# Strided attention on one core: storing some head groups alone, and scoring group 0 ahead of the second cast

## The chip, the cores and the metric

One core of one Trainium2 chip. The metric is the device time in microseconds (us) of one execution; medians of several fast runs are quoted. An execution is counted as slow, and left out, when it took over 1.5% longer than the fastest one of the same kernel. "The span" is the profiled part of it, some 2 us shorter than the time. Ratios between kernels are the mean time of one kernel's fast runs over that of the other's fast runs of the same rounds, so they are not quite the ratio of the medians quoted. The calls ran on different chips; times are best compared within one call.

## The reference

Every query attends to 16 fixed keys, those at positions 0, 64, 128 and so on:

```python
batch, heads, seq, dim = (8, 12, 1024, 64)      # float32, stride = 64
for i in range(seq):
    attend_positions = np.arange(0, seq, stride)
    q = Q[:, :, i:i + 1, :]
    k = K[:, :, attend_positions, :]
    v = V[:, :, attend_positions, :]
    scores = np.einsum('bhqd,bhkd->bhqk', q, k) * scale
    weights = ...softmax of scores...
    result[:, :, i, :] = np.einsum('bhqk,bhkd->bhqd', weights, v)[:, :, 0, :]
```

Q is 25.2 MB and is read once; the result is 25.2 MB and is written once. The kernel moves some 51 MB and computes little.

## The kernel before

The 96 heads are handled in 24 groups of four, 1 MB of Q and 1 MB of result each. All transfers are issued from one queue (SP), in program order. Ten input buffers let loads 0 to 9 go ahead; load g+10 needs the buffer of group g. A group is cast to bf16 (half on GpSimd, half on ScalarE), transposed on VectorE, scored on TensorE, exponentiated on ScalarE, multiplied with V on TensorE, and scaled by the reciprocal sums on VectorE (five eighths of it) and on ScalarE and GpSimd (the last three eighths).

```python
def cast(g):
    ...
    nc.gpsimd.tensor_copy(out=qb[g][:, 0:half], in_=qn[g][:, 0:half])
    nc.scalar.copy(qb[g][:, half:], qn[g][:, half:])

def store(g, groups, a):                 # a: parity of the head
    o = out_sb[g][a : P : 2]             # every second partition: 64 rows
    _copy(nc,
          _ap_with(out, [[16 * D, 64], [2 * SD, 2 * groups], [1, 16 * D]],
                   g * HG * SD + a * SD),
          _ap_with(o, [o.ap[0], [1, 1], [1, 32 * groups * D]]))

key_rows(0)
cast(0)
cast(1)
keys(0, 0)
transpose(0)
scores(0)
keys(0, 1)
... # V, transpose(1), cast(2)
for g in range(NG):
    ... # outputs(g), and the steps ahead of the next groups
    if g >= NG - 2:
        for a in range(2):
            store(g, 1, a)
    elif g % 2 == 1:
        for a in range(2):
            store(g - 1, 2, a)           # two groups at once, one parity: 16 KiB reads
            if g - 1 + a + QBUFS < NG:
                load(g - 1 + a + QBUFS)
```

Two groups lie side by side in one output buffer, so a store of one parity of both reads 16 KiB from each of 64 partitions. A store of one group reads 8 KiB pieces.

The softmax here doesn't subtract the row's maximum and nothing guards it: scores larger than these inputs give would overflow.

Of the kernel before, what the change touches and what calls it, by code (L numbers as in the profile page):

```python
# [12 lines left out]
BF16 = mybir.dt.bfloat16  # L13
# [6 lines left out]
def _ap_with(ap: bass.AP, new_ap, extra_offset: int = 0) -> bass.AP:  # L20
    return dataclasses.replace(
        ap, ap=[list(p) for p in new_ap], offset=ap.offset + extra_offset
    )


def _copy(nc, out: bass.AP, in_: bass.AP):

    sides = [
        mybir.BassSymbolicTensorAccessPattern(
            ap=side.ap, dtype=side.dtype, bass_ap=side,  # L30
            is_dma=True, for_custom_bir_dma=True,
        )
        for side in (in_, out)
    ]
    return nc.sync.add_instruction(  # L35
        mybir.InstDMACopy(
            name=nc.get_next_instruction_name(), engine=mybir.EngineType.SP,
            ins=sides[:1], outs=sides[1:], queue="qSPDynamicHW",
            mode="Copy",
        )  # L40
    )
# [9 lines left out]
def kernel(  # L51
# [8 lines left out]
    nc = tc.nc  # L60

    B, H, S, D = Q.shape
# [3 lines left out]
    P = 128  # L66
    HG = 4
    NG = B * H // HG
    NC = NG // 2
    SD = S * D  # L70
    KW = P + NK
    assert B * H == NG * HG and S == 1024 and D == 64 and NK == 16
    QBUFS = 10
    OBUFS = 4

    const = ctx.enter_context(tc.tile_pool(name="const", bufs=1))
# [16 lines left out]
    def load(g):  # L93
        qn[g] = qn_pool.tile([P, 32 * D], FP32, name="qn", tag="qn")
        n = P if g < 2 else 32
        _copy(nc, qn[g], _ap_with(Q, [[HG * SD // n, n], [1, HG * SD // n]], g * HG * SD))
# [18 lines left out]
    for c in range(2):  # L115
        for a in range(2):
            for e in range(2):
                nc.gpsimd.tensor_copy(
                    out=perm_v[:, c, a, :, e], in_=id_v[:, c, :, a]
# [4 lines left out]
    w_bufs = []  # L124
    for i in range(3):
        w = const.tile([P, 8, P], BF16, name=f"w{i}")
# [6 lines left out]
        out=slot_i, in0=iota_p, scalar1=4, scalar2=3,  # L133
# [6 lines left out]
        out=s_sel, in0=col4, scalar1=slot_f, scalar2=None, op0=ALU.is_equal  # L140
# [15 lines left out]
    def key_rows(m):  # L156
        part = slice(4 * m, 4 * m + 4)
        nc.scalar.copy(k_bf[:, part], k_raw[:, part])  # L158
        nc.vector.transpose(  # L159
            k_r[:, part].rearrange("p n d -> p (n d)").bitcast(I32),  # L160
            k_bf[:, part].rearrange("p n d -> p (n d)").bitcast(I32),
        )


    def keys(m, c):
        for s in range(4):
            src, dst, col = 32 * (2 * c + s % 2), 32 * (2 * (s % 2) + s // 2), NK + 32 * s
            op = nc.vector.tensor_copy if m == 0 and s >= 2 else nc.scalar.copy
            op(  # L169
                k_t[dst : dst + 32, 8 * m + c : 8 * m + 8 : 2, :, col : col + NK],  # L170
                k_r[src : src + 32, 4 * m : 4 * m + 4].rearrange(
                    "p n (a k f) -> p a n f k", a=2, f=2
                )[:, s // 2],
            )


    def value_rows(n):
        for c in range(2):
            vp = psum_sc.tile([P, NC // 2, D], FP32, name="vp", tag="sc")
            nc.tensor.matmul(  # L180
                vp, lhsT=perm_v[:, c].rearrange("p a b e k -> p (a b e k)"),
                rhs=v_bf[:, 6 * n : 6 * n + 6], start=True, stop=True,
            )
            nc.vector.tensor_copy(out=v_rep[:, 6 * n : 6 * n + 6, c], in_=vp)  # L184

    qb, qt, wt, vb, rec, out_sb, out_2 = {}, {}, {}, {}, {}, {}, {}


    def values(g):
        vb[g] = v_bufs[g % 3]  # L190
        nc.gpsimd.tensor_tensor(  # L191
            out=vb[g][:, 0 : 4 * D].rearrange("p (s d) -> p s d", s=4), in0=mask,
            in1=v_rep[:, g // 2, g % 2].unsqueeze(1).to_broadcast([P, 4, D]),
            op=ALU.mult,
        )

    def cast(g):
        qb[g] = qb_pool.tile([P, 32 * D], BF16, name="qb", tag="qb")
        half = 16 * D
        nc.gpsimd.tensor_copy(out=qb[g][:, 0:half], in_=qn[g][:, 0:half])  # L200
        nc.scalar.copy(qb[g][:, half:], qn[g][:, half:])  # L201

    def transpose(g):
        qt[g] = qt_pool.tile([P, 32 * D], BF16, name="qt", tag="qt")
        nc.vector.transpose(qt[g].bitcast(I32), qb[g].bitcast(I32))  # L205

    def scores(g):
        sc = psum_sc.tile([P, 512], FP32, name="sc", tag="sc")
        q = qt[g]
        for e in range(2):  # L210
            for f in range(2):
                nc.tensor.matmul(  # L212
                    sc, lhsT=k_t[:, g, f, NK * (1 - e) : NK * (1 - e) + P],
                    rhs=_ap_with(
                        q, [q.ap[0], [D, 8], [16 * D, 2], [2, 32]],
                        extra_offset=8 * D * e + f,
                    ),
                    start=e + f == 0, stop=e + f == 2,
                )
        w = wt[g] = w_bufs[g % 3]  # L220
        for a in range(2):
            wa = w[64 * a : 64 * a + 64]
            nc.scalar.activation(  # L223
                out=_ap_with(wa, [wa.ap[0], [P, 8], [4, 32], [2, 2]], extra_offset=a),
                in_=sc[64 * a : 64 * a + 64].rearrange("p (t x q) -> p t q x", t=8, x=2),
                func=AF.Exp, bias=0.0, scale=scale,
            )


    def outputs(g, c):  # L230
        if c == 0:
            if g % 2 == 0:
                out_2[g // 2] = out_pool.tile(
                    [P, 2, 4, 8, D], FP32, name="out_sb", tag="out_sb"
                )
            out_sb[g] = out_2[g // 2][:, g % 2]
            rec[g] = rec_pool.tile([P, 8, 4], FP32, name="rec", tag="rec")
        i0, n = ((0, 3), (3, 2), (5, 3))[c]
        ps = psum_o.tile([P, 3, 512], FP32, name="o_ps", tag="o")
        for i in range(n):  # L240
            nc.tensor.matmul(  # L241
                ps[:, i, 0 : 4 * D + 4], lhsT=wt[g][:, i0 + i], rhs=vb[g],
                start=True, stop=True,
            )
        r = rec[g][:, i0 : i0 + n]
        o = ps[:, 0:n, 0 : 4 * D].rearrange("p i (s d) -> p i s d", s=4)
        to = out_sb[g][:, :, i0 : i0 + n].rearrange("p s i d -> p i s d")
        by = r.unsqueeze(3).to_broadcast([P, n, 4, D])
        nc.vector.reciprocal(r, ps[:, 0:n, 4 * D : 4 * D + 4])  # L249
        if c < 2:  # L250
            nc.vector.tensor_tensor(out=to, in0=o, in1=by, op=ALU.mult)  # L251
        else:
            nc.scalar.copy(to, o)  # L253
            nc.gpsimd.tensor_tensor(out=to, in0=to, in1=by, op=ALU.mult)  # L254


    def store(g, groups, a):
        o = out_sb[g][a : P : 2]
        _copy(
            nc,  # L260
            _ap_with(
                out, [[16 * D, 64], [2 * SD, 2 * groups], [1, 16 * D]],
                g * HG * SD + a * SD,
            ),
            _ap_with(o, [o.ap[0], [1, 1], [1, 32 * groups * D]]),
        )

    key_rows(0)
    cast(0)
    cast(1)  # L270
    keys(0, 0)
    transpose(0)
    scores(0)
    keys(0, 1)
    nc.vector.tensor_copy(out=v_bf, in_=v_raw)
    transpose(1)
    value_rows(0)
    values(0)
    values(1)
    cast(2)  # L280
    def ahead(g):
        if g + 2 < NG:
            transpose(g + 2)
        if g + 1 < NG:
            scores(g + 1)
        if g + 2 < NG:
            values(g + 2)
        if g + 3 < NG:
            cast(g + 3)

    for g in range(NG):
        if g > 0:
            ahead(g)
        for c in range(3):
            outputs(g, c)
        if g == 0:
            ahead(g)
        if g in (1, 5):
            key_rows(g // 4 + 1)
        if g in (2, 3, 6, 7):  # L300
            keys(g // 4 + 1, g % 4 - 2)
        if g == 4:
            value_rows(1)
        if g >= NG - 2:
            for a in range(2):
                store(g, 1, a)
        elif g % 2 == 1:
            for a in range(2):
                store(g - 1, 2, a)
                if g - 1 + a + QBUFS < NG:  # L310
                    load(g - 1 + a + QBUFS)
# [33 lines left out]
```

## Time and profile before

| | before |
|---|---|
| time, median (range) | 132.21 us (132.01 to 132.62), 3 runs |
| span | 130.1 us |
| DMA engines busy, mean of 16 | 96% |
| busiest compute engine | VectorE, 68% |

How to read the profile lines: in the rows of stretches by time, the columns are start and end of the stretch, its length, then busy time and instructions of PE, weight loads, DVE, ACT and POOL, then the granted TensorE clock, the DMA share and GB/s. This view books the bytes of a packet where the packet starts, so a share slightly above 1 means busy throughout. In timeline lines: start, duration, engine, source line, operation, output<-input. For a DMA line, the duration is that of the issue, not that of the transfer. The lines of the kernel before stand in the prediction below.

Beside the views I use the trace's records of single DMA packets, which have a start, a duration and a size, but no number of their engine. Loads from load 2 on consist of 32 KiB packets (median 1219 ns), pair stores of 16 KiB packets (616 ns), and lone stores of 8 KiB packets (311 ns). From them I work out two figures for each run, over the packets that start between 29 and 66 us:

- **idle**: the time in which fewer than 16 packets are in flight, the missing ones summed and divided by 16;
- **excess**: each packet's duration less the median of its size as given here, summed and divided by 16. It is what slow packets cost.

### The profile page before, as it was taken

How to read it: one execution, taken by the hardware profiler on the slowest of the kernel's cores; microseconds unless marked ns; L12 is line 12 of the kernel's file. 1: busy time of each engine (PE TensorE's matmuls, PEld its weight loads, DVE VectorE, ACT ScalarE, POOL GpSimd, SP SyncE). 2: the span in 40 equal slices, each digit the busy share in tenths (PEclk: the TensorE clock that was granted, in tenths of full speed). 3: DMA queues.
4: the chain of work that ended last, by engine and by line, in shares of the span. 5: the costliest groups of instructions: out<-in, count | busy, mean ns of one | idle time of the engine just before them, and what ended most of it. 6: DMA issues, size and time to landing. Idle time of an engine off the chain costs nothing.

```text
span 130.1 us, 1201 instructions
## 1 busy us (share of the span) xinstructions
PE 65.9 (51%) x292; PEld 30.6 (24%) x292; DVE 88.8 (68%) x167; ACT 86.3 (66%) x120; POOL 80.1 (62%) x89
## 2 busy tenths in 40 slices
PE   0000669376885647743667764666646377450000
PEld 0000223133342313321332331333323223210000
DVE  6964565469688968796898797979798865660000
ACT  3133365967899896999978789797979683431000
POOL 8933074918657875785878969696988755244000
PEclk9999999955558996799975699999999955865555
DMA  3999989997979999999999999999999999999991
GB/s 70 353 322 463 474 343 473 423 383 322 322 267 451 388 443 436 393 438 446 408 428 453 398 438 453 388 438 453 393 433 458 388 438 428 423 421 428 403 406 50
DMA packets 6535, 51.20 MB, mean 393 GB/s; under 512 B 3904, under 2 KB 3904, under 8 KB 3904
## 3 DMA queue, kind: packets, MB, share of 16 engines
q1 hardware_dynamic: 6528, 51.12, 96.0%
q8 instruction: 2, 0.03, 0.1%
q14 instruction: 5, 0.04, 0.1%
HBM read 25.95 MB, written 25.17 MB: 393 GB/s over the span
## 4 chain that ended last, share of the span: by engine, by line
DMA 35%; POOL 23%; issue 17%; DVE 5%; ACT 4%; PE 4%; SPq 1%; POOLq 1%; DVEq 0%; ACTq 0%
DMA qn<-in_Q_dram 35%; POOL out_sb L254 9%; POOL qb L200 8%; POOL v L191 5%; DVE out_sb L251 3%; PE sc L212 3%; ACT qb L201 2%; DVE qt L205 1%; POOLq L340 1%; ACT out_sb L253 1%; PE o_ps L241 1%; DVE rec L249 1%; ACT k_t L169 1%; ACT w L223 1%; SPq L35 1%
## 5 line engine op out<-in xcount | busy, mean ns | idle before, releaser
L241 PE MATMUL o_ps<-v,w 128*128 128x260 bf16 x192 | 39.0, 325 | 36.0 <-DVE out_sb L251 31.8
L254 POOL TENSOR_TENSOR out_sb<-out_sb,rec 128x768 f32<-128x768 f32 x24 | 35.3, 1471 | 29.4 <-ACT out_sb L253 29.4
L251 DVE TENSOR_TENSOR out_sb<-o_ps,rec 128x768 f32<-128x768 f32 (+1 forms) x48 | 39.6, 824 | 1.9 <-DVE rec L249 0.3
L212 PE MATMUL sc<-qt,k_t 128*128 128x512 bf16 x96 | 33.2, 481 | 14.0 <-ACT k_t L169 13.5
L223 ACT ACTIVATE w<-sc 64x512 bf16<-64x512 f32 x48 | 35.4, 737 | 5.1 <-PE sc L212 4.7
L205 DVE STREAM_TRANSPOSE qt<-qb 128x1024 int32<-128x1024 int32 x24 | 29.6, 1232 | 12.8 <-POOL qb L200 7.8
L241 PEld LDWEIGHTS <-w 128*128 128x128 bf16 x192 | 19.2, 111 | 59.9 <-DVE out_sb L251 40.4
L201 ACT CAST qb<-qn 128x1024 bf16<-128x1024 f32 x24 | 25.1, 1045 | 7.6 <-DMA qn<-in_Q_dram 7.0
L253 ACT COPY out_sb<-o_ps 128x768 f32<-128x768 f32 x24 | 19.2, 798 | 14.6 <-DVE rec L249 14.3
L200 POOL CAST qb<-qn 128x1024 bf16<-128x1024 f32 x24 | 24.9, 1037 | 5.2 <-DMA qn<-in_Q_dram 5.2
L249 DVE RECIPROCAL rec<-o_ps 128x12 f32<-128x12 f32 (+1 forms) x72 | 15.1, 210 | 7.4 <-PE o_ps L241 6.7
L191 POOL TENSOR_TENSOR v<-mask,v_rep 128x256 bf16<-128x256 bf16 x24 | 16.1, 669 | 3.9 <-DVE v_rep L184 3.9
L212 PEld LDWEIGHTS <-k_t 128*128 128x128 bf16 x96 | 10.9, 114 | 24.9 <-ACT k_t L169 13.5
L169 ACT COPY k_t<-k_r 32x128 bf16<-32x128 bf16 x20 | 5.9, 294 | 0.2
L129 POOL MEMSET k_t<- 128x4608 bf16 x1 | 3.9, 3936 | 0.0
L184 DVE CAST v_rep<-vp 128x384 bf16<-128x384 f32 x4 | 2.1, 538 | 2.0 <-PE vp L180 2.0
L158 ACT CAST k_bf<-k_raw 128x256 bf16<-128x256 f32 x3 | 1.2, 407 | 3.1 <-DMA k_raw<-in_K_dram 3.1
L139 DVE TENSOR_SCALAR s_sel<-col,slot_f 128x4 bf16<-128x4 int16 x1 | 2.5, 2545 | 0.1
L159 DVE STREAM_TRANSPOSE k_r<-k_bf 128x128 int32<-128x128 int32 x3 | 0.9, 308 | 2.3 <-ACT k_bf L158 2.3
L180 PE MATMUL vp<-v_bf,perm_v 128*128 128x384 bf16 x4 | 1.5, 413 | 0.6 <-DVE v_rep L184 0.6
L158 ACT ACT_TABLE_LOAD x1 | 1.3, 1283 | 0.7 <-PEq L326 0.7
L123 DVE MEMSET k_t<- 128x1152 uint32 x1 | 1.0, 1018 | 1.0 <-PEq L326 1.0
(17 smaller groups left out, 6.6 us busy)
## 6 DMA issues: line engine op xcount, KB each, us to landing
qn<-in_Q_dram SPq DMA_DIRECT2D x24, 1024.0 KB, 14.1
out_dram<-out_sb SPq DMA_DIRECT2D x22, 1024.0 KB, 13.6
out_dram<-out_sb SPq DMA_DIRECT2D x4, 512.0 KB, 9.2
k_raw<-in_K_dram SPq DMA_DIRECT2D x1, 384.0 KB, 4.3
v_raw<-in_V_dram SPq DMA_DIRECT2D x1, 384.0 KB, 7.4
```

The source lines that it names most:

```text
L169: op(k_t[dst : dst + 32, 8 * m + c : 8 * m + 8 : 2, :, col : col + NK], k_r[src : src + 32, 4 * m : 4 * m + 4].rearrange("p n (a k f) -> p ...
L191: nc.gpsimd.tensor_tensor(out=vb[g][:, 0 : 4 * D].rearrange("p (s d) -> p s d", s=4), in0=mask, in1=v_rep[:, g // 2, g % 2].unsqueeze(1).t ...
L200: nc.gpsimd.tensor_copy(out=qb[g][:, 0:half], in_=qn[g][:, 0:half])
L201: nc.scalar.copy(qb[g][:, half:], qn[g][:, half:])
L205: nc.vector.transpose(qt[g].bitcast(I32), qb[g].bitcast(I32))
L212: nc.tensor.matmul(sc, lhsT=k_t[:, g, f, NK * (1 - e) : NK * (1 - e) + P], rhs=_ap_with(q, [q.ap[0], [D, 8], [16 * D, 2], [2, 32]], extra_ ...
L223: nc.scalar.activation(out=_ap_with(wa, [wa.ap[0], [P, 8], [4, 32], [2, 2]], extra_offset=a), in_=sc[64 * a : 64 * a + 64].rearrange("p (t ...
L241: nc.tensor.matmul(ps[:, i, 0 : 4 * D + 4], lhsT=wt[g][:, i0 + i], rhs=vb[g], start=True, stop=True,)
L249: nc.vector.reciprocal(r, ps[:, 0:n, 4 * D : 4 * D + 4])
L251: nc.vector.tensor_tensor(out=to, in0=o, in1=by, op=ALU.mult)
L253: nc.scalar.copy(to, o)
L254: nc.gpsimd.tensor_tensor(out=to, in0=to, in1=by, op=ALU.mult)
```

## The change

The intent is to give the DMA queue its first stores earlier. The first four groups, and the last two, are stored alone; and the keys and scores of group 0 are recorded ahead of cast 1, which has to wait for load 1. Nearly every store is one DMA of 1 MB before and after (only the last four were halves), so no DMA is split; what changes is when its data are ready. Lone groups lay the attention weights out differently, so the pairs need three zeroed weight buffers of their own.

```diff
+    def alone(g):
+        return g < 4 or g >= NG - 2
...
-        w = wt[g] = w_bufs[g % 3]
+        w = wt[g] = (w_bufs if alone(g) else w_pair)[g % 3]
+        wa_pos, wa_step = ([[2, 32], [1, 2]], 64) if alone(g) else ([[4, 32], [2, 2]], 1)
...
+    def store(g):                       # 128 rows, 8 KiB reads
+        o = out_sb[g]
+        _copy(nc,
+            _ap_with(out, [[16 * D, P], [2 * SD, 2], [1, 16 * D]], g * HG * SD),
+            _ap_with(o, [o.ap[0], [1, 1], [1, 32 * D]]))
...
     key_rows(0)
+    keys(0, 0)
     cast(0)
+    ...three w_pair tiles, memset on GpSimd...
+    transpose(0)
+    keys(0, 1)
+    scores(0)
     cast(1)
-    keys(0, 0)
-    transpose(0)
-    scores(0)
-    keys(0, 1)
... (transpose(1) moves behind values(1))
-        if g >= NG - 2:
-            for a in range(2):
-                store(g, 1, a)
+        if alone(g):
+            store(g)
+            if g + QBUFS < NG:
+                load(g + QBUFS)
         elif g % 2 == 1:
             for a in range(2):
-                store(g - 1, 2, a)
+                store_two(g - 1, a)     # as before
```

More of the change, by code (lines that the diff above doesn't have):

```diff
@@ L223, in scores @@
             nc.scalar.activation(
-                out=_ap_with(wa, [wa.ap[0], [P, 8], [4, 32], [2, 2]], extra_offset=a),
+                out=_ap_with(wa, [wa.ap[0], [P, 8], *wa_pos], extra_offset=a * wa_step),
                 in_=sc[64 * a : 64 * a + 64].rearrange("p (t x q) -> p t q x", t=8, x=2),
@@ L254, in outputs, with store_two @@
             nc.gpsimd.tensor_tensor(out=to, in0=to, in1=by, op=ALU.mult)
-    def store(g, groups, a):
+    def store(g):
+        o = out_sb[g]
+        _copy(
+            nc,
+            _ap_with(out, [[16 * D, P], [2 * SD, 2], [1, 16 * D]], g * HG * SD),
+            _ap_with(o, [o.ap[0], [1, 1], [1, 32 * D]]),
+        )
+    def store_two(g, a):
         o = out_sb[g][a : P : 2]
@@ L261, in store @@
             _ap_with(
-                out, [[16 * D, 64], [2 * SD, 2 * groups], [1, 16 * D]],
+                out, [[16 * D, 64], [2 * SD, 4], [1, 16 * D]],
                 g * HG * SD + a * SD,
             ),
-            _ap_with(o, [o.ap[0], [1, 1], [1, 32 * groups * D]]),
+            _ap_with(o, [o.ap[0], [1, 1], [1, 64 * D]]),
         )
     key_rows(0)
+    keys(0, 0)
     cast(0)
+    w_pair = []
+    for i in range(3):
+        w = const.tile([P, 8, P], BF16, name=f"w_pair{i}")
+        nc.gpsimd.memset(w, 0.0)
+        w_pair.append(w)
+    transpose(0)
+    keys(0, 1)
+    scores(0)
     cast(1)
-    keys(0, 0)
-    transpose(0)
-    scores(0)
-    keys(0, 1)
     nc.vector.tensor_copy(out=v_bf, in_=v_raw)
-    transpose(1)
     value_rows(0)
@@ L279 @@
     values(1)
+    transpose(1)
     cast(2)
```

## The prediction

> **What bounds the kernel now.** I began with the page: busy shares, the 40 slices, the chain that ended last; then asked for the stretches by time, the timeline, and the DMA queue's own waits. No compute engine is above 68% of the span, but the 16 DMA engines are at 96%:
>
> ```profile
> PE 65.9 (51%) x292; PEld 30.6 (24%) x292; DVE 88.8 (68%) x167; ACT 86.3 (66%) x120; POOL 80.1 (62%) x89
> ...
> GB/s 70 353 322 463 474 343 473 423 383 322 322 267 451 388 443 436 393 438 446 408 428 453 398 438 453 388 438 453 393 433 458 388 438 428 423 421 428 403 406 50
> ...
> q1 hardware_dynamic: 6528, 51.12, 96.0%
> ```
>
> So it is bound by moving 51.12 MB: at the 426 GB/s of the long steady stretch (below) that alone is 120.0 us of the 130.1 us span. The interest is in the other 10. The GB/s row has one hole in the middle: slices 10 to 12 (each 3.25 us) at 322, 322 and 267. The stretches by time, with the last two columns DMA share and GB/s, place it:
>
> ```profile
> 9.00:30.00 21.00, 11.72 (x38) 4.87 (x39) 12.04 (x21) 12.16 (x18) 9.19 (x10) 0.91 1.04 437
> 30.00:32.00 2.00, 0.74 (x5) 0.22 (x3) 1.93 (x5) 1.94 (x3) 1.94 (x3) 0.50 0.31 131
> 32.00:39.00 7.00, 6.11 (x22) 2.73 (x21) 5.32 (x9) 5.98 (x12) 3.83 (x4) 0.50 1.01 311
> 39.00:126.00 87.00, 47.33 (x233) 22.80 (x231) 63.06 (x120) 63.46 (x86) 58.14 (x56) 0.83 1.00 426
> ```
>
> Two different faults lie there. From 30 to 32 us the DMA share is 0.31: the engines are idle. From 32 to 39 us the share is 1.01, but only 311 GB/s move: the engines are busy and slow. The timeline of the DMA queue says why the first one exists:
>
> ```profile
> 2.63 9.71 SPq L35 DMA_DIRECT2D qn<-in_Q_dram  x9
> 30.36 0.63 SPq L35 DMA_DIRECT2D out_dram<-out_sb  x1
> 31.09 0.54 SPq L35 DMA_DIRECT2D qn<-in_Q_dram  x1
> ...
> 39.74 0.59 SPq L35 DMA_DIRECT2D out_dram<-out_sb  x1
> ```
>
> All ten loads that the input buffers allow are issued by 12.34 us. Nothing follows until 30.36 us, because the first store waits for both groups of pair 0, and load 10 stands behind that store in the same queue. In the trace's packet records the last packets of load 9 end between 30.68 and 31.21 us, and the first store packet starts at 31.65. What held the store is the last multiply of group 1 on GpSimd, 28.86 to 30.33 us:
>
> ```profile
> 28.86 1.47 POOL L254 TENSOR_TENSOR out_sb<-out_sb,rec 128x768 f32<-128x768 f32 x1 [2.94 <-ACT out_sb L253]
> ```
>
> From 39 us to the end nothing starves. The chain that ended last runs over GpSimd early, and over loads (35% of the span) later; the waits of the DMA queue for GpSimd after 39 us cost nothing, as the queue has work in hand.
>
> **What the Trainium skill says.** "DMA: Bandwidth & Descriptors", section "Queues, rings and completion order": on each DMA engine descriptors are consumed in ring order. The trace agrees: the loads of the first stage finish one after another, about 2.49 us apart, so a store issued at 20 us is not carried out at 20 us but is ready when load 9 ends. "HBM Reference", section "Specifications (TRN2)": a core streaming alone measures about 425 GB/s, bounded by its 16 DMA engines; the trace has 426. So there is no faster steady rate to win, only holes to close. "Perfetto Trace Analysis", section "DMA Optimizations": splitting DMAs may let some start sooner. That is what storing groups alone does. I found no page that explains a stretch of busy but slow packets.
>
> **The change, part by part.**
>
> *Reads of 8 KiB.* Stores of groups 0 to 3 read 128 rows of 8 KiB where pairs read 64 rows of 16 KiB. In the packet records the median 8 KiB packet takes 311 ns (they are what the last four stores use) and the median 16 KiB packet 616 ns. A group has 64 x 16 KiB, 4 for each engine: 4 x (2 x 311 - 616) = 24 ns. Four groups: +0.1 us. Groups 22 and 23 keep 8 KiB reads, in two issues instead of four: 0.
>
> *Three more zeroed buffers.* Pairs and lone groups lay their weights out differently, so there are three new w buffers, zeroed on GpSimd. The memset of k_t there takes 3.94 us for 4608 columns, 0.855 ns each; 3 x 1024 columns make 2.6 us. They stand between cast 0 (ends 8.78 us) and cast 1, which waits for load 1 until 11.89 us. 8.8 + 2.6 = 11.4: hidden.
>
> *Keys and scores of group 0 ahead of cast 1.* Before, the first score matmul starts at 13.47 us because ACT does cast 1 (11.87 to 12.91, on load 1) ahead of the keys. After, ACT does the keys at about 7.4, cast 0 to about 9.0; the transpose (1.25) ends at about 10.3, and the remaining keys at about 10.7. Scores start near 10.5, 3 us earlier. Values of group 0 on GpSimd still come after cast 1 (12.9) and v_rep (about 13.8), so output matmuls of group 0 start near 14.5, not 17.08: 2.6 us earlier. Before, its last multiply ended at 21.23 + 1.47 = 22.7, so it ends near 20.
>
> *Store 0 and load 10 alone.* The store can go at about 20 us instead of 30.36, ten before the loads run out. Load 10 follows at once. Store 0 and load 10 are 2.1 MB, 4.9 us at 426 GB/s: work until about 30.9 + 4.9 = 35.8. Store 1 is needed by then; it was ready at 30.3 in the kernel before and should be at about 28. Each further group adds 4.9 us of DMA work against 4.5 to 4.9 us between the last multiplies (28.86, 33.73, 38.24, 42.87). Pair 4/5 was ready at 48.15 and is needed at 30.9 + 4 x 4.9 = 50.5, so the return to pairs does not starve either. Idle DMA goes.
>
> *The sum.* Against 426 GB/s the kernel before loses 2 x (1 - 131/426) = 1.4 us in the idle stretch, and 7 x (1 - 311/426) = 1.9 us in the slow one; together 3.3. Nothing else that bounds changes. If both vanish: 132.2 - 3.3 + 0.1 = 129.0. If only the idle one does: 132.2 - 1.4 + 0.1 = 130.9.
>
> **The rivals.** (A) *The slow packets come from restarting dry engines.* For: 16 KiB packets take up to 1306 ns there, about twice the median, and it starts 1.2 us after the restart; packets also run slow (8 KiB in 700 to 800 ns) at 3.8 us, just after the DMA first starts. Against: the first two packets of every engine after the restart run at full speed. Then both parts go, near 129.0.
> (B) *They come from the first writes to the output, whenever those start.* For: the dip follows the first stores, and it hits loads behind them as well; no reads alone show it. Against: later stores go to equally fresh addresses at full speed. Then the slow stretch only moves: near 130.9, or 131.3 if the window boundaries of mine gave the idle part too much.
> (C) *The granted clock or the engines' load slow the DMA.* The clock is 0.50 in that stretch; but it is also 0.50 at 69 to 72 us with 448 GB/s, so I dismiss it.
> (D) *Compute becomes the bound between groups 1 and 5.* Margins of 2 to 8 us as above speak against it; a miss would give back a microsecond.
> (E) *The end is ragged.* The last stores end between 126.5 and 128.6 us, one engine trailing others by up to 2 us. The change does not touch its cause, and it can move the time by 0.5 us either way.
>
> **Range and chances.** I give A and B about equal weight: (129.0 + 130.9) / 2 is 129.95, and I lean a little to the faster side because a partial remedy of the slow stretch is possible even under B, as loads are then mixed in sooner: 129.8. Half a microsecond either side of the two cases makes 128.4 to 131.6. The 2% border is at 129.57: under A about two in three fall below, under B one in ten, so faster 0.39, same 0.59, slower 0.02. Being slower by 2.6 us would need a new hole as large as the present one, and I see none.
>
> **What would show it.** Right: the first store issued near 20 us with load 10 just behind; no stretch between 3 and 125 us with a DMA share under 0.9; first scores near 10.5 us; the span's end earlier by what the hole loses. A stretch around 31 to 37 us at the full rate decides for A; one of busy share near 1 at about 300 GB/s decides for B. Wrong: store 0 issued after 25 us, a second hole near 36 or 50 us because outputs come late, or 8 KiB packets well above 311 ns when mixed with loads.

## The result

| | before | after |
|---|---|---|
| time, median (range) | 132.22 us (132.01 to 132.62), 4 runs | 129.05 us (128.95 to 129.44), 4 runs |
| ratio, 95% interval | | 0.9762 (0.9732 to 0.9793) |
| span | 130.1 us | 127.3 us |
| end of the last DMA packet | 128.63 us | 126.02 us |
| idle, excess (29 to 66 us) | 0.93, 2.13 us | 0.11, 0.20 us |

The changed kernel is 2.4% faster. A second and a third set of runs of it, below, gave 0.9795 (0.9777 to 0.9813) and 0.9770 (0.9740 to 0.9800), so that a gain of 2% is not clear of the noise in these two. The profiled execution of the kernel before took 131.88 us, that of the changed one 129.10: the profiles account for 2.8 us, not for the whole difference of the medians. The stretches by time of the kernel after, over the hole and past it:

```profile
9.00:30.00 21.00, 13.07 (x44) 5.40 (x44) 15.12 (x25) 12.36 (x19) 13.80 (x15) 0.92 1.03 433
30.00:32.00 2.00, 1.45 (x9) 0.57 (x6) 1.97 (x5) 1.69 (x5) 0.84 (x1) 1.00 0.74 307
32.00:39.00 7.00, 3.42 (x18) 1.61 (x19) 5.31 (x12) 6.82 (x12) 5.31 (x6) 0.97 1.03 437
39.00:123.00 84.00, 46.87 (x224) 22.26 (x222) 60.60 (x114) 60.28 (x82) 55.77 (x53) 0.80 1.01 426
```

The stretch from 32 to 39 us went from 311 to 437 GB/s, and the steady rate stayed at 426. The 0.74 from 30 to 32 us is not a hole: by the packet records at least 16 packets are in flight from 29 to 32 us, but few start there. The queue's timeline, and group 0 on its way to the first store:

```profile
2.63 9.61 SPq L35 DMA_DIRECT2D qn<-in_Q_dram  x9
20.61 0.63 SPq L35 DMA_DIRECT2D out_dram<-out_sb  x1
21.34 0.55 SPq L35 DMA_DIRECT2D qn<-in_Q_dram  x1
27.96 0.59 SPq L35 DMA_DIRECT2D out_dram<-out_sb  x1
...
45.84 0.59 SPq L35 DMA_DIRECT2D out_dram<-out_sb  x1
```

```profile
8.63 2.73 POOL L287 MEMSET w_pair<- 128x1024 bf16 x3
10.42 1.87 PE L215 MATMUL sc<-qt,k_t 128*128 128x512 bf16 x4 [10.42 <-DVE qt L208]
11.80 1.36 POOL L203 CAST qb<-qn 128x1024 bf16<-128x1024 f32 x1 [0.44 <-DMA qn<-in_Q_dram]
...
19.11 1.47 POOL L259 TENSOR_TENSOR out_sb<-out_sb,rec 128x768 f32<-128x768 f32 x1 [2.86 <-ACT out_sb L258]
```

Store 0 is issued at 20.61 us instead of 30.36, ten ahead of the end of load 9 (30.41 to 31.08 us over the engines), and load 10 stands right behind it. The memsets are over before cast 1's data are in. They were not quite free: a copy of keys on VectorE, started at 10.40 us, took 1.04 us instead of 0.22 and ended 0.08 us after the last memset. This cost the DMA queue nothing here; the dry spell in the middle, below, shows a profile in which it did.

One line of the table of groups was not in my working, the exponentials, by layout:

```profile
L228 ACT ACTIVATE w_pair<-sc 64x512 bf16<-64x512 f32 x36 | 26.6, 738 | 1.9 <-PE sc L215 1.6
...
L228 ACT ACTIVATE w<-sc 64x512 bf16<-64x512 f32 x12 | 7.1, 591 | 3.7 <-PE sc L215 3.6
```

The lone layout writes neighbouring columns and takes 591 ns, not 738, for the same number of elements. It takes 1.8 us off ScalarE in all, which bounds nothing here.

### The profile page after: what moved, and what is told of

Read it like the earlier page. It is cut to its first block, busy times and chain, and to the rows that moved or that the text cites. A ratio compares the mean times of both kernels' runs of the same rounds, so it can differ in the third digit from the quotient of the medians.

```text
span 127.3 us, 1203 instructions
## 1 busy us (share of the span) xinstructions
PE 64.8 (51%) x292; PEld 29.9 (24%) x292; DVE 89.3 (70%) x167; ACT 84.5 (66%) x120; POOL 83.0 (65%) x92
## 4 chain that ended last, share of the span: by engine, by line
POOL 39%; issue 25%; DVE 11%; DMA 6%; ACT 4%; PE 4%; POOLq 1%; DVEq 0%
POOL qb L203 15%; POOL out_sb L259 14%; POOL v L194 10%; DMA out_dram<-out_sb 6%; DVE qt L208 3%; DVE out_sb L256 3%; PE sc L215 2%; DVE s_sel L139 2%; ACT qb L204 2%; PE o_ps L246 2%; ACT out_sb L258 1%; POOLq L360 1%; DVE w L127 1%; ACT w L228 1%; DVE rec L254 1%
## 5 line engine op out<-in xcount | busy, mean ns | idle before, releaser
L259 POOL TENSOR_TENSOR out_sb<-out_sb,rec 128x768 f32<-128x768 f32 x24 | 35.3, 1471 | 30.1 <-ACT out_sb L258 30.1
L246 PE MATMUL o_ps<-v,w_pair 128*128 128x260 bf16 x144 | 27.7, 305 | 28.1 <-DVE out_sb L256 24.3
L215 PE MATMUL sc<-qt,k_t 128*128 128x512 bf16 x96 | 32.1, 468 | 10.4 <-DVE qt L208 10.4
L228 ACT ACTIVATE w_pair<-sc 64x512 bf16<-64x512 f32 x36 | 26.6, 738 | 1.9 <-PE sc L215 1.6
L246 PEld LDWEIGHTS <-w_pair 128*128 128x128 bf16 x144 | 13.7, 106 | 44.4 <-DVE out_sb L256 30.3
L246 PE MATMUL o_ps<-v,w 128*128 128x260 bf16 x48 | 11.1, 367 | 9.0 <-DVE out_sb L256 8.3
L228 ACT ACTIVATE w<-sc 64x512 bf16<-64x512 f32 x12 | 7.1, 591 | 3.7 <-PE sc L215 3.6
L246 PEld LDWEIGHTS <-w 128*128 128x128 bf16 x48 | 5.2, 120 | 16.6 <-DVE out_sb L256 10.8
L287 POOL MEMSET w_pair<- 128x1024 bf16 x3 | 2.7, 947 | 0.0
```

The lines of the kernel that those rows point to most:

```text
L215: nc.tensor.matmul(sc, lhsT=k_t[:, g, f, NK * (1 - e) : NK * (1 - e) + P], rhs=_ap_with(q, [q.ap[0], [D, 8], [16 * D, 2], [2, 32]], extra_ ...
L228: nc.scalar.activation(out=_ap_with(wa, [wa.ap[0], [P, 8], *wa_pos], extra_offset=a * wa_step), in_=sc[64 * a : 64 * a + 64].rearrange("p ...
L246: nc.tensor.matmul(ps[:, i, 0 : 4 * D + 4], lhsT=wt[g][:, i0 + i], rhs=vb[g], start=True, stop=True,)
L259: nc.gpsimd.tensor_tensor(out=to, in0=to, in1=by, op=ALU.mult)
```

## The experiments

The theory after the result: the whole gain is that the DMA engines no longer run dry. Running dry costs twice, once as idle time and once as a stretch of slow packets after the restart. Rivals: the slow stretch belonged to the first writes to the output; or to the parity pairs; or the earlier scores are worth something of their own.

### Each part alone

The first run takes the order alone, in the kernel before (transpose(1) moves here too):

```diff
     key_rows(0)
+    keys(0, 0)
     cast(0)
+    transpose(0)
+    keys(0, 1)
+    scores(0)
     cast(1)
-    keys(0, 0)
-    transpose(0)
-    scores(0)
-    keys(0, 1)
...
```

> The kernel before with the new order of keys and scores alone; every store stays a parity pair. Main theory (the loss was only that the first store came after the loads had run out, and dry engines restart slowly): group 1 ends at about 27.9 us as in the changed kernel, pair 0 is issued at about 28.0, ahead of the loads' end at 30.4 to 31.1; no stretch from 30 to 39 us under 400 GB/s; 129.1 us. Rival (the first stores must be lone, because 16 KiB pair reads or two parity stores as the first writes are what ran slowly): idle stretch gone, slow stretch of 5 to 6 us stays, about 131.0 us.

The second takes the lone stores alone: the changed kernel with the order of before.

> The changed kernel with the old order of casts, keys and scores; the lone stores stay. Main theory: group 0 ends at about 22.7 us, store 0 is issued then, 8 us ahead of the loads' end; 129.1 us, the same as the changed kernel, so each of the two parts would have been enough alone. Rival (the earlier start of scores is worth something of its own): between 129.6 and 131 us.

| | time | ratio to before (95%) | idle, excess |
|---|---|---|---|
| order alone | 130.03 us | 0.9836 (0.9821 to 0.9850) | 0.12, 1.13 us |
| lone stores alone | 129.94 us | 0.9837 (0.9804 to 0.9870) | 0.12, 0.66 us |
| changed kernel | 129.51 us | 0.9795 (0.9777 to 0.9813) | 0.10, 0.18 us |

Each part alone takes the idle time away and gives about four fifths of the gain of that call. The parts are two remedies for one fault, not two gains. But neither reached the 129.1 us that the main theory expected, and the lone stores came out inside the range of the rival that gave the earlier scores a worth of their own (129.6 to 131). The packet records speak for slow packets instead: some remain, from 32 to 36 us with the order alone and from 52 to 56 us with the lone stores alone. With the order alone:

```profile
32.00:39.00 7.00, 2.92 (x18) 1.45 (x18) 5.43 (x12) 6.80 (x14) 5.57 (x6) 0.96 1.04 396
```

In these two, the store concerned was issued some 2 us ahead of its turn. In the changed kernel it is 4 us or more. The times differ as the excess does (0.48 us of excess and 0.43 us of time between the lone stores and the changed kernel), but the intervals of these two overlap, so this rival is made unlikely and not excluded.

### Loads ahead of the first stores

Loads 10 and 11 need only casts 0 and 1, so they need not stand behind a store:

```diff
+    load(QBUFS)
+    load(QBUFS + 1)
     for g in range(NG):
...
-                if g - 1 + a + QBUFS < NG:
+                if g > 1 and g - 1 + a + QBUFS < NG:
                     load(g - 1 + a + QBUFS)
```

> The kernel before with nothing changed but that loads 10 and 11 are issued ahead of the first stores (they wait for casts 0 and 1 alone, so they can go at about 13 us). The loads then run to about 36 us and the first store, still issued near 30.4 us as a pair, is carried out behind them. Main theory: no dry stretch, no slow one, 129.2 us, perhaps 0.3 more since pair 1 at 39.7 us comes just as pair 0's stores end at 41. Rival (first writes are slow whenever they come as pairs): slow stretch at 36 to 42 us, 130.9 us.

130.89 us, ratio 0.9903 (0.9886 to 0.9920): a miss in the time. The packet records say where it went. The first stores, pair 0 of both parities from 35.3 to 41 us, ran at full speed: their 16 KiB packets took 616 ns, although they were the first writes and pairs. This refutes the rival of the first writes. But pair 1 then came just in time: its first store was issued at 39.24 us, with only the second store of pair 0 still under way, and started at about 40.5 us. Idle was only 0.19 us, yet the excess was 1.87 us, with 16 KiB packets at up to 1245 ns from 41.7 to 43 us and slow 32 KiB packets behind them. The stretches by time of this kernel:

```profile
32.00:39.00 7.00, 4.83 (x22) 2.12 (x20) 5.51 (x11) 6.46 (x14) 4.34 (x4) 0.83 0.97 410
39.00:46.00 7.00, 5.33 (x20) 2.42 (x21) 5.68 (x12) 6.39 (x9) 4.90 (x6) 0.66 1.06 350
```

The slow stretch moved to where the queue was nearly empty; the lower rate stands in the row of 39 to 46 us.

### A hold that held nothing

> The changed kernel with the stores of groups 4 and 5 and the loads 14 and 15 held back until after group 6 (issue near 51 us, not 45.8), so that the DMA engines run dry in the middle, at 50 to 51.6 us, for 1 to 2 us, long after the first writes. If any restart of dry engines brings a slow stretch: idle about 1.4 us plus about 1.9 us of slow packets (16 KiB packets near 1250 ns) from 53 to 59 us, about 132.3 us. If the slow stretch of the kernel before belonged to the first writes or the first phase only: the idle time alone, about 130.5 us, packets at 611 to 616 ns right after the restart.

The edit put the stores of pair 4/5 behind group 6 in the program. On SP a store waits only for the data that it reads, and no other transfer stood ahead of it, so it went out at 45.75 us as ever: 129.51 us and no dry spell. The run tested neither theory. It serves as a second run of the changed kernel, used in the table above.

### Loads further ahead

```diff
+    for g in range(QBUFS, QBUFS + 3):
+        load(g)
...
         if g == 0:
             ahead(g)
+            load(QBUFS + 3)
...
-                if g - 1 + a + QBUFS < NG:
-                    load(g - 1 + a + QBUFS)
+                if g > 1 and g + 1 + a + QBUFS < NG:
+                    load(g + 1 + a + QBUFS)
```

> The kernel before with loads 10 to 13 issued ahead of the first stores and every later load two groups earlier; all stores stay parity pairs. So far the slow packets came in this order: 2.0 us of excess packet time where the store came after the engines were dry (before), 1.7 where it came about 1.5 us ahead of its turn (loads 10 and 11 ahead), 0.7 and 0.4 where it came 2 to 2.5 us ahead (order alone, lone stores alone), none where it came 4 us ahead (changed kernel). If the short lead is what counts: here every pair is issued 6 us or more ahead of its turn, no slow stretch, about 129.6 us. If engines in step (ends of one transfer within 0.6 us over the 16 engines) followed by a pair store and a load are what counts: slow stretch of 1 to 2 us of excess at pair 1, near 46 to 52 us, about 131 us.

130.00 us, ratio 0.9849 (0.9801 to 0.9897), idle 0.11 and excess 0.92 us. The large slow stretch is gone, as the lead theory said, but a mild one is left, from 45.7 to 48.4 us, in the third store in a row (packets of 700 to 970 ns), and that store had been issued six microseconds ahead. So a short lead is not the only condition for slow packets. The rival of this run, engines in step, had expected 1 to 2 us of excess and about 131 us; the result lies between the two and settles neither. What else counts stays open.

### Dry on purpose, with lone stores, and in the middle

To hold a store back in fact, it must stand in the queue behind another that has to wait. First with lone stores:

```diff
         if alone(g):
-            store(g)
-            ...
+            for h in {0: (), 1: (), 2: (2, 0, 1)}.get(g, (g,)):
+                store(h)
+                if h + QBUFS < NG:
+                    load(h + QBUFS)
```

> The changed kernel, but the stores of groups 0 and 1 stand behind the store of group 2 (issue near 32.7 us), so the engines run dry at 30.4 to 31.1 us for about 2.8 us and restart with lone stores of 8 KiB reads. If any restart of dry engines brings a slow stretch: 2.8 us idle plus about 2 us of excess packet time in the 6 us after the restart, near 134.0 us. If slow packets need the parity pairs: idle time alone, packets at 311 ns, near 131.9 us.

134.54 us over the three fast runs (a fourth, 136.65 us, was counted as slow), ratio 1.0179 (1.0126 to 1.0232). Idle 3.52 us, excess 1.61 us: 8 KiB packets took 540 to 669 ns from 36.0 to 37 us, and half of the 32 KiB packets of the load behind them 1581 to 2051. So the slow stretch does not need parity pairs. The same with pair 4/5 behind pair 6/7, in the middle of the run:

```diff
+            for h in {5: (), 7: (7, 5)}.get(g, (g,)):
                 for a in range(2):
-                    store_two(g - 1, a)
+                    store_two(h - 1, a)
...
```

> The changed kernel, but the stores of pair 4/5 stand behind those of pair 6/7, which need group 7 (issue near 55 us): the engines run dry at 50 to 51.6 us for 4 to 5.5 us, in the middle, and restart with a parity pair long after the first writes. If a restart with a parity pair brings the slow stretch: about 5 us idle and 2 us of excess, near 136 us. If the slow stretch belonged to the first phase of the run: 5 us idle alone, near 134 us. (The run e4 was meant to do this, but its stores wait only for their own groups and went out unmoved; it counts as a second run of the changed kernel.)

The profiled run was counted as slow (138.46 us); the three fast ones took 136.30, 136.51 and 136.97 us, and the ratio is 1.0344 (1.0290 to 1.0397). The profile is used for what happens around the dry spell only. Its stretches by time:

```profile
39.00:46.00 7.00, 5.12 (x21) 2.33 (x22) 5.80 (x12) 6.22 (x9) 5.11 (x6) 0.76 0.99 418
46.00:53.00 7.00, 3.35 (x21) 1.77 (x20) 5.99 (x12) 5.78 (x11) 4.76 (x5) 1.00 0.63 261
53.00:59.00 6.00, 3.36 (x18) 1.51 (x17) 3.86 (x8) 5.83 (x11) 4.47 (x5) 0.92 0.11 45
59.00:66.00 7.00, 4.97 (x19) 2.11 (x16) 5.40 (x9) 5.91 (x8) 5.00 (x5) 0.58 1.01 318
```

The engines fell idle between 50 and 52.2 us and stayed so until 58.6 us, and from 59 to 66 us they were busy at 318 GB/s: the picture of the kernel before at 30 to 39 us, 27 us later and long after the first writes. Idle was 8.28 us and excess 2.02 us; the fourth 16 KiB packet of each engine took 1240 to 1295 ns.

The trace shows what set this execution apart from its early stage on. Two lines of GpSimd's timeline, then one of VectorE's:

```profile
7.57 1.04 POOL L203 CAST qb<-qn 128x1024 bf16<-128x1024 f32 x1 [1.03 <-DMA qn<-in_Q_dram]
8.55 2.73 POOL L287 MEMSET w_pair<- 128x1024 bf16 x3
...
7.35 4.00 DVE L169 COPY k_t<-k_r 32x128 bf16<-32x128 bf16 x2
```

The second of these two copies of keys on VectorE started at 7.58 us, 13 ns after cast 0 on GpSimd, and took 3.77 us instead of 0.22: it ended at 11.36 us, 0.08 us after the memsets that follow the cast. In the ten profiles in which the copy started before the cast, it took 0.22 us; in the other two in which it started after, 1.07 us (loads ahead, without memsets) and 3.64 us (lone stores alone). Here the first scores came at 12.69 us, not 10.42, store 0 at 22.88, not 20.61, and the held pair's stores as much later. In the fast runs, which were not profiled, the dry spell was therefore probably about 2.3 us shorter. An estimate from these figures: 129.05 us, 5.9 us more idle and 1.8 us more excess make 136.7 us; without the slow stretch 134.9. The fast runs took 136.3 to 137.0, so they too speak for the slow stretch.

### Restart with loads

In the kernel before, one packet for each engine was stored after the dry spell, then loads 10 and 11, then the rest:

```diff
+        elif g == 1:
+            store(0, 2, 0, 0, 16)       # 16 of the 64 rows
+            load(QBUFS)
+            load(QBUFS + 1)
+            store(0, 2, 0, 16, 64)
+            store(0, 2, 1)
         elif g % 2 == 1:
```

> The kernel before, where the first store is cut: 16 rows of pair 0 (one packet for each engine), then loads 10 and 11, then the other 48 rows and the odd parity. The engines run dry as before (about 1 us near 31 us) but restart with loads. If any transfer after a dry spell runs slowly: load packets of 1500 to 2500 ns, not 1240, from 33 to 38 us, about 2 us of excess, 132.2 us as before. If it takes a run of stores behind the dry spell: loads at 1240 ns, at most the idle time lost, near 130.5 us.

132.93 us, ratio 1.0059 (1.0029 to 1.0089). The 16 KiB packets of the small store took 1173 to 1320 ns, and the packets of the loads from 1416 to 2339 ns where slow, the last of them 7 us after the restart. Idle 1.45 us, excess 2.73 us:

```profile
32.00:39.00 7.00, 5.64 (x24) 2.66 (x24) 5.50 (x11) 5.75 (x11) 3.78 (x5) 0.76 0.99 318
```

So loads run slowly after a dry spell too, and changing what comes first is no remedy. The time is 0.7 us above what the first theory expected (132.2): both the idle time and the excess were larger than in the kernel before.

### Is the layout of pairs worth its code, and is anything left?

All groups lone (the test `alone` returns True):

> The changed kernel with every group stored alone, 128 rows of 8 KiB. By the packet medians (311 ns for 8 KiB, 616 for 16 KiB) 18 more groups cost 18 x 24 ns = 0.4 us: 129.5 us. Rival (parity pairs cost something in slow packets): 129 us or less, with no packets over 1.1 times their median where pairs 4/5 come in.

129.34 us, ratio 0.9790 (0.9748 to 0.9832), no worse than the changed kernel beyond the noise. The mean of its 8 KiB packets is 312.9 ns, and that of the changed kernel's 16 KiB packets 617.3. The expected cost of 0.4 us is within what the intervals allow and is not shown. Lastly all lone, the new order, and loads two groups earlier, beside the changed kernel again, five rounds:

> All groups lone, the new order, and every load two groups earlier than in the changed kernel: the largest lead of any kernel here. If what the lead gives is used up once nothing runs dry: no better than the changed kernel, 129.1 us give or take 0.4, ratio to it within 0.5%. If some slow packets are still left to win: 128.5 us or less.

> The changed kernel itself, once more and on the same chip as the two others, to compare with: 129.1 to 129.5 us, ratio to before 0.976 to 0.980, no stretch between 9 and 120 us with more than 0.3 us of excess packet time.

129.42 us, ratio 0.9793 (0.9767 to 0.9820), against 129.09 us, ratio 0.9770 (0.9740 to 0.9800). Once nothing runs dry, a larger lead brings nothing. No kernel beats the changed one; all lone comes level, and could do with simpler code (as run, it still zeroed the pair buffers that it did not use).

## Why the prediction was right or wrong

- **The bound and the hole: right.** The steady rate is 426 GB/s before and after, and the gain is the hole at 30 to 39 us. Of the 2.61 us by which the last packet ends earlier, idle accounts for 0.82 (0.93 - 0.11) and excess for 1.93 (2.13 - 0.20), with 0.1 given back elsewhere. The same sum, taken against the changed kernel, gives the end of the last packet within 0.15 us for the six fast profiles of experiments that lost more than 0.4 us (0.5 to 5 us later), and 0.7 us too late for the slow one. Where nothing was lost, that end still varies from 125.8 to 126.5 us, so differences of half a microsecond are not to be read closely.
- **The early phase: right, step by step, but for one wait.** First scores at 10.42 us (predicted 10.5), memsets 2.73 us (2.6), done before cast 1 (that they hold a VectorE copy up was not foreseen: 1.04 us for 0.22, and 3.77 in one profile, as above), store 0 at 20.61 (about 20), store 1 at 27.96 (about 28), pair 4/5 at 45.84 (needed by 50.5). No second hole came.
- **The size: in the range, the middle 0.75 us too high.** The prediction gave "A and B about equal weight". That weighing is the step that failed: both parts of the loss went, as A had it. The figure that A carried, 129.0 us, is what was measured (129.05), though partly by luck: its idle term, 1.4 us read from window rates, was 0.93 us by the packet records, of which 0.82 went, while its slow term, 1.9, was right (1.93). It had put 0.59 on "within 2%", and the result is just past 2%. The evidence that was there for A, slow packets soon after the DMA's first start, counted for more than I let it; that the first two packets of each engine ran at full speed was no argument against A, as in the middle dry spell they did so too. The range was wide enough for A and B alike and did not decide between them.
- **Rival B, first writes: refuted** by the loads-ahead run, where the first writes ran at 616 ns, and by the middle dry spell.
- **Rival C, the clock: rejected, as predicted.** After the lone dry spell, packets were slow from 35.5 us with the granted clock at 1.00 until 38.5 us.
- **Rival D did not occur. Rival E, the ragged end, is still there:** fewer than 16 packets are in flight from 123.5 us on, and the last one ends at 126.0 us.
- **8 KiB reads, +0.1 us:** too small to be seen; with all groups lone even 0.4 was not.
- **What I did not see:** that each part alone would nearly do. The working had both dates (22.7 for group 0 in the old order, 28 for group 1 in the new), and either lies ahead of 30.7.
- **Open:** why packets are slow for some 6 us after the engines have been dry. The loss did not grow with the dry spell: 2.13, 2.73, 1.61 and 2.02 us of excess with 0.93, 1.45, 3.52 and 8.28 us of idle. Slow stretches also came with nearly no idle time (1.87, 1.13, 0.92, 0.66 us), so a dry spell brought one in all four kernels that had it, but it is not necessary. Whether what was missing was transfers in hand, or engines that are out of step with each other, no run here separates.

## What to carry to other kernels

Where a kernel is bound by DMA, look for the date at which the prefetched loads run out, and have the first store, with the next load behind it, in the queue some microseconds before. Count a dry spell at more than its own length: here 1.6 to 2.7 us of slow packets came on top, with no growth from dry spells of 1 to 8 us, and they hide under a busy share near 1, so read GB/s beside it. To hold or to free a transfer in one in-order queue, ask what stands ahead of it there, not where it stands in the program.

## What the Trainium skill lacked or had wrong

- "DMA: Bandwidth & Descriptors" has nothing on a slow stretch after the DMA engines have been dry: 16 KiB packets at up to 1320 ns instead of 616, 8 KiB at up to 669 instead of 311, over some 6 us, 1.6 to 2.7 us lost in four runs.
- The same page gives rates by transfer size, none for loads and stores mixed: 32 KiB load packets took 1240 to 1246 ns while only loads ran, and 1219 (median) when stores ran beside them.
- "Perfetto Trace Analysis", section "DMA Optimizations", counsels larger DMAs, with batches of 4 KB or 8 KB as its example, and gives no size beyond which nothing more is gained. Reads of 16 KiB against 8 KiB in SBUF gained nothing that could be measured here (ratios to before 0.9790 with 8 KiB throughout, 0.9762 with pairs in the middle, and the intervals overlap).
- No page was found that gives the cost of the exponential by output layout: 591 ns with neighbouring columns, 738 ns with every second one, for 64 x 512 elements.
